# A streaming-encoder step on one core: norms behind a block's second group, w_in scaled on GpSimd from the second group on, latents' transposes in the next block

## The chip, the cores and the metric

The kernel runs on one core of a Trainium2 chip. The metric is the device time of one execution in microseconds, and the time of a kernel is the median of its runs. A core has a matrix engine (TensorE, PE in the profile, with its weight loads as PEld), a vector engine (VectorE, DVE), an activation engine (ScalarE, ACT), a general engine (GpSimd, POOL) and a queue engine that issues DMAs (SyncE, SP). Each engine works through its own instructions in program order and waits on semaphores for the others.

## The reference, cut to what matters

One layer of a hybrid encoder: a norm, one input projection, two token mixers (a gated linear recurrence and latent attention), an output projection, then a feed-forward part. 2048 prompt tokens and 32 tokens of a running stream go through it together. The first half of `trunk_layer` is what the change touches:

```python
xn = rms_norm(x, g_pre_mix)
proj = jnp.einsum('btd,dc->btc', xn, w_in)
x_lru, gate, c_q, c_kv, k_r = jnp.split(
    proj, [LRU_W, 2 * LRU_W, 2 * LRU_W + Q_LORA, 2 * LRU_W + Q_LORA + KV_LORA], axis=-1)

xc, conv_new = causal_conv(x_lru, conv0, conv_w, conv_b)
h, h_last = rglru(xc, h0, w_a, b_a, w_i, b_i, lam)
y_lru = h * jax.nn.gelu(gate)
...
q = jnp.einsum('btr,rhe->bthe', rms_norm(c_q, g_q), w_uq)
ckv_new = rms_norm(c_kv, g_kv)
krope_new = apply_rope(k_r, cos, sin)
```

with

```python
def rms_norm(x, g):
    xf = x.astype(jnp.float32)
    y = xf * lax.rsqrt(jnp.mean(xf * xf, axis=-1, keepdims=True) + EPS)
    return (y * g.astype(jnp.float32)).astype(x.dtype)

# rglru, per channel c and token t:
#   a = exp(-8 * sigmoid(gate r) * softplus(-lam))
#   bx = sqrt(1 - a^2) * sigmoid(gate i) * xc
#   h[t] = a[t] * h[t-1] + bx[t]
```

The model width is 1024 (KD = 8 pieces of 128), the recurrence is 512 wide (G = 4 pieces), c_q is 256, c_kv 128 and k_r 32 wide.

## The kernel before

The program has four stages: `front` (the projection, conv and recurrence, lines 227 to 673), attention, the output projection, and the feed-forward part `mlp`. The last is the longest: the page's lines with `x_hi`, `h_hi` and `w_hl` are its.

**Front** works through 8 blocks of TB = 256 tokens, the last with the 32 stream tokens beside it (288). All products are in float32 in three passes of a rounded high part and a low rest (`mm3`, L159, L160, L161; `split` makes the pair, L147, L149, L152). In a block, PE does in this order: eight groups m=0..7 (each 24 matmuls of 128 x 256, weights `wa_hi`, `wa_lo`, tokens `xt_hi`, `xt_lo`) into a PSUM tile `ps` from a pool `pp` of three buffers; the products of the latents into `psr` (two tiles of the same pool); and the gates, eight sets of three matmuls into `psg`.

The norm isn't applied to the tokens but to the product. Per block two `row` tiles are loaded, squared and summed (ACT L306), turned into `rstd` (POOL L167), spread (`rb`, DVE L309), multiplied with a unit matrix on PE (L320, tile `rps`) and copied by ACT into `r_all` (L324): a row of 256 factors on all partitions. The function `stats` does this. `evac` takes a group's `ps` out and frees its buffer: for m < 4 DVE multiplies with `r_all` into `xl` (L550) and the conv follows (one step on POOL, L556, three on DVE, L561); for m >= 4 DVE multiplies into `gt` (L568), and after m=7 ACT applies the gelu. A group's evacuation can't start before `r_all` is there.

After the groups: `operand` splits the conv's result (`xch`, `xcl`), `latents` takes c_q, c_kv and k_r out of `psr`, with norms (`qn` L389, `kv` L392), and hands back a function `lat_t`, which transposes them on PE (four transposes, L418, into `tps`, a single PSUM buffer), has ACT copy them into `sp_t` (L420) and stores that. `gates` ends in sigmoids on ACT (L456). `recur` runs on ACT (exp L468, tanh L470, Square L471, Sqrt L475, with table loads between), DVE (L472, L483, scans L486) and POOL (L480); `mix` multiplies `gt` with the scan's result (DVE L498) and stores `ylru_d`.

**What sets the order.** PE's order is the order in which the code issues its work; the other engines' orders are made by a scheduler from that program. Before, `gates` of a block issues `stats` of the next block after its third set (j=2) and the first `lat_t` after its fifth (j=4); the second `lat_t` comes after group m=0 of the next block. For block 0 there is no block before: its `rstd` is made while w_in is loaded, and `stats` stands after group m=2; `held` keeps the groups until then.

**Loading w_in** happens during block 0. `load_wa(m)` loads one group's 128 x 1024 weights and has to multiply them by the norm's gain `g_pre`. For m >= 4 GpSimd does that in one instruction (L332), and ACT and DVE split the result in one instruction each (L147, L152). For m < 4 ACT (L341) and DVE (L342) do both at once in eight pieces of 128 x 128 each.

In `mlp`, two PSUM tiles are taken from the pool `pm` and never used ahead of the first products (L1521).

Of the kernel before, what the change touches and what calls it, by code (L numbers as in the profile page):

```python
# [18 lines left out]
KD = 8  # L19
# [15 lines left out]
TB = 256  # L35
# [73 lines left out]
class Step:  # L109
# [117 lines left out]
    def front(self, ca, cb):  # L227
# [3 lines left out]
        with ExitStack() as ctx:  # L231
# [39 lines left out]
            def size(b):  # L271
                return TB + (S if b == self.nb - 1 else 0)
# [24 lines left out]
            def row(i, tag=None):  # L297
                m = 128 if i < self.nt else S
                xr = (tp if tag else rp).tile([128, D], F32, name="xrow_t", tag=tag or "xr")
                nc.sync.dma_start(out=xr[:m], in_=A["x_rows"][i * 128 : i * 128 + m] if m == 128 else A["xs_rows"])  # L300
                return xr
# [10 lines left out]
            def stats(b, rbs=None):  # L312

                n = size(b)
                rps = pr.tile([128, 512], F32, name="rps", tag="rps")
                for t in range((n + 127) // 128):
                    m = min(128, n - t * 128)
                    i = 2 * b + t
                    rb = rbs[t] if rbs else rstd(i, row(i))
                    nc.tensor.matmul(  # L320
                        out=rps[:, t * 128 : t * 128 + m], lhsT=rb[:m], rhs=self.ident[:m, :m], start=True, stop=True
                    )
                r = t2.tile([128, TB + S], F32, name="r_all", tag="r_all")
                nc.scalar.activation(out=r[:, :n], in_=rps[:, :n], func=AF.Copy)  # L324
                return r


            def load_wa(m):
                raw = tp.tile([128, KD, 128], F32, name="wa_raw_t", tag=("ig", "rg", "xcl", "xch")[m % 4])
                nc.sync.dma_start(out=raw, in_=A["w_a"][m])  # L330
                if m >= 4:
                    nc.gpsimd.tensor_tensor(  # L332
                        out=raw, in0=raw, in1=self.g_pre[:, :, None].to_broadcast([128, KD, 128]), op=ALU.mult
                    )
                    self.split(wa_hi[m], wa_lo[m], raw, nc.scalar, nc.vector)
                else:
                    return lambda k: scale_wa(m, k, raw)
# [108 lines left out]
            def gates(w, we, xch, xcl, between={}):  # L446
                rg = tp.tile([128, G, xpad], F32, name="rg", tag="rg")
                ig = tp.tile([128, G, xpad], F32, name="ig", tag="ig")
                for i, (dst, bias) in enumerate(((rg, self.b_a), (ig, self.b_i))):
                    for g in range(G):  # L450
                        ps = pg.tile([128, 512], F32, name="psg", tag="psg")
                        j = i * G + g
                        self.mm3(
                            ps[:, :we], wg_hi[:, j], wg_lo[:, j], xch[:, g, :we], xcl[:, g, :we], True, True
                        )
                        nc.scalar.activation(  # L456
                            out=dst[:, g, :w], in_=ps[:, :w], func=AF.Sigmoid, bias=bias[:, g : g + 1]
                        )
                        if j in between:
                            between[j]()  # L460
                return rg, ig
# [50 lines left out]
            late = []  # L512
            xl_prev = None
            nxt = None
            for b in range(self.nb):
                end = b == self.nb - 1
                n = size(b)
                w = TB + (S + 3 if end else 0)
                we = w + (w % 2)
                if b == 0:  # L520
                    piece = load_wa(0)
                    xh, xlo = load_x(0, 4, piece)
                    piece = load_wa(1)
                    for k in range(KD):
                        piece(k)
                    rows0 = [row(0), row(1, "gt")]
                    rbs = [rstd(i, xr) for i, xr in enumerate(rows0)]
                    for m in (2, 3):
                        piece = load_wa(m)
                        for k in range(KD) if piece else ():  # L530
                            piece(k)
                    r_all = None
                else:
                    xh, xlo = nxt
                    r_all = r_next
                xl = t2.tile([128, G, 3 + xpad], F32, name="xl", tag="xl")
                if b == 0:
                    nc.vector.memset(xl[:, :, 0:3], 0.0)
# [37 lines left out]
                for m in range(8):  # L576
                    if b == 0 and 2 <= m < 6:
                        load_wa(m + 2)
                    if b == 0 and m == 7:
                        load_wb()  # L580
                        wg_raw = t2.tile([128, 2 * G, 128], F32, name="wg_raw", tag="sp_t", bufs=1)
                        nc.sync.dma_start(out=wg_raw, in_=A["w_gate"].rearrange("p a g c -> p (a g) c"))
                        with self.tc.issue_after(self.split(wg_hi, wg_lo, wg_raw, nc.scalar, nc.vector).ins):
                            decay()
                    ps = pp.tile([128, 512], F32, name="ps", tag="ps")
                    for k in range(KD):
                        self.mm3(
                            ps[:, :n], wa_hi[m][:, k], wa_lo[m][:, k], xh[:, k, :n], xlo[:, k, :n],
                            k == 0, k == KD - 1,
                        )  # L590
                    if late and m == 0:
                        late.pop(0)()
                    held.append((m, ps))
                    if r_all is None and m == 2:
                        r_all = stats(0, rbs)
                    if r_all is not None:
                        for x in held:
                            evac(*x)
                        held.clear()
                    if end and m == 6:  # L600

                        hv = recur(end, w, xc, *gates(w, we, *operand(xc, w, we)))
# [23 lines left out]
                if not end:  # L626
                    xch, xcl = operand(xc, w, we)
# [6 lines left out]
                if end:  # L634
                    self.kdone = min(2, (self.n - TB) // 512)
                    t0 = self.nt - TB // 128
                    first = []

                    def early_q(x, ps):

                        self.mul_q(ps, self.uq0, 512 * x)
                        qf = t2.tile([128, 512], F32, name="qf", tag="sp_t", bufs=1)
                        q = [self.k_hi[2][:, 512 * y : 512 * y + 512] for y in (2 * x, 2 * x + 1)]
                        self.first_q[0, x] = self.put_q(ps, 512 * x, qf, *q)

                    def early_k(x, ps):
                        self.mul_k(ps, x, uk)
                        self.put_k(ps, 0, x)

                    self.first_q = {}  # L650
                    t14 = latents(t0, 0, xh, xlo, None)
                    if self.kdone:
                        early_q(0, pr.tile([128, 512], F32, name="psq", tag="rps"))
                        early_k(0, pt.tile([128, 4, 128], F32, name="psk", tag="tps").rearrange("p a b -> p (a b)"))
                    ts = latents(self.nt, TB, xh, xlo, None)
                    t14()
                    t15 = latents(t0 + 1, 128, xh, xlo, None)
                    ts()
                    if self.kdone == 2:
                        early_k(1, pg.tile([128, 512], F32, name="psk", tag="psg"))  # L660
                        early_q(1, pp.tile([128, 512], F32, name="psq", tag="ps"))
                    t15()
                else:
                    sp_t = t2.tile([128, 4, TB], F32, name="sp_t", tag="sp_t", bufs=1)
                    for t in range(n // 128):
                        late.append(latents(2 * b + t, 128 * t, xh, xlo, sp_t))
                    rn = []
                    others = [lambda: rn.append(stats(b + 1)), lambda: late.pop(0)()]
                    rg, ig = gates(w, we, xch, xcl, dict(zip((2, 4), others)))
                    r_next = rn[0]  # L670
                    while len(late) > 1:
                        late.pop(0)()
                    mix(b, end, n, w, xl, gt, recur(end, w, xc, rg, ig))

    def alloc_a(self, ca):
# [829 lines left out]
    def mlp(self):  # L1505
# [11 lines left out]
        g_post = self.cp.tile([128, D], F32, name="g_mlp_post", tag="keep")  # L1517
        nc.sync.dma_start(out=g_post, in_=A["g_rows"][:, D : 2 * D].to_broadcast([128, D]))
        bank = lambda: pm.tile([128, 512], F32, name="ps", tag="ps")

        bank(), bank()  # L1521
        fill, fin = [], []
        turn = [0]
        done = {}
# [385 lines left out]
```

## Time and profile before

| what | us |
|---|---|
| median of 3 runs | 2483.93 |
| the runs | 2483.0 to 2487.58 |
| the profiled execution | 2484.81 |
| its span | 2483.0 |
| end of the front stage in it, about | 352 |

The profile is one execution. A row of the timeline has a start, a duration, an engine, a line, the operation, what it writes and reads, and how often it runs in a row; a bracket tells how long the engine was idle before it and what released it. A row of the waits tells engine, tile and line, what it waited for, and then microseconds in total, times and the longest. A row of the windows has a stretch, its length, and the busy time of PE, PEld, DVE, ACT and POOL with instruction counts, then the clock granted to TensorE (1.00 is full), the DMA engines' share and GB/s.

### The profile page before, as it was taken

The page shows a single profiled execution, that of the slowest core. Times are in us where ns is not written, and L with a number is a line of the kernel's source. Part 1 is how long each engine was busy: PE and PEld are TensorE (multiplying, and loading weights), DVE is VectorE, ACT ScalarE, POOL GpSimd, SP SyncE. Part 2 cuts the span into 40 slices and gives each one's busy share as a digit, 9 for nine tenths or more (in the row PEclk, how much of TensorE's full clock was granted, in tenths as well). Part 3 has the DMA queues.
Part 4 walks back from the last instruction along what each step waited for, and adds up shares of the span by engine and source line. Part 5 has one row for each costly group of instructions (what it writes and reads, how often), then busy time and mean ns, then how long its engine had stood idle before and what let it go on. Part 6 is the DMA issues. An engine that isn't in the chain of part 4 may idle for free.

```text
span 2483.0 us, 44188 instructions
## 1 busy us (share of the span) xinstructions
PE 2391.4 (96%) x15287; PEld 2274.4 (92%) x15287; DVE 1788.7 (72%) x3573; ACT 1549.9 (62%) x3473; POOL 624.2 (25%) x1040
## 2 busy tenths in 40 slices
PE   7999989999999999999999999999999999999998
PEld 7889978888888787777999999999999999999997
DVE  7646589898888884465877777676677777667676
ACT  6554558788788783343666766466676656666564
POOL 4443366777577682111000000000000000000000
PEclk9999999999999999999999999999999999999999
DMA  6522211333334325495666887676678767667773
GB/s 211 146 73 75 79 49 50 84 84 87 86 86 123 99 59 164 121 288 171 210 221 227 282 261 242 210 239 232 215 268 261 241 218 236 226 230 267 236 240 131
DMA packets 325489, 436.45 MB, mean 176 GB/s; under 512 B 32336, under 2 KB 242544, under 8 KB 325264
## 3 DMA queue, kind: packets, MB, share of 16 engines
q1 hardware_dynamic: 324624, 433.10, 54.8%
q8 instruction: 120, 1.97, 0.3%
q14 instruction: 105, 0.86, 0.1%
q10 hardware_dynamic: 640, 0.52, 0.1%
HBM read 309.63 MB, written 123.90 MB: 175 GB/s over the span
## 4 chain that ended last, share of the span: by engine, by line
PE 71%; DVE 10%; ACT 6%; issue 5%; POOL 4%; DMA 2%; SPq 0%; ACTq 0%; DVEq 0%; POOLq 0%
PE ps L159 17%; PE ps L160 17%; PE ps L161 17%; PE po L995 4%; PE ptp L979 4%; PE pss L159 2%; PE pss L160 2%; PE pss L161 2%; DVE xc L561 1%; ACT w_hl L147 1%; ACT p L913 1%; DVE w_hl L152 1%; DVE hv L486 1%; DVE c L1619 1%; POOL xc L556 1%
## 5 line engine op out<-in xcount | busy, mean ns | idle before, releaser
L159 PE MATMUL ps<-x_hi,w_hl 128*128 128x352 f32 (+1 forms) x1344 | 432.4, 322 | 5.0 <-DVE x L1387 3.3
L160 PE MATMUL ps<-x_lo,w_hl 128*128 128x352 f32 (+1 forms) x1344 | 432.4, 322 | 0.0
L159 PE MATMUL ps<-h_hi,w_hl 128*128 128x352 f32 (+1 forms) x1344 | 432.3, 322 | 0.0
L161 PE MATMUL ps<-x_hi,w_hl 128*128 128x352 f32 (+1 forms) x1344 | 431.5, 321 | 0.0
L160 PE MATMUL ps<-h_lo,w_hl 128*128 128x352 f32 (+1 forms) x1344 | 430.4, 320 | 0.1
L161 PE MATMUL ps<-h_hi,w_hl 128*128 128x352 f32 (+1 forms) x1344 | 430.4, 320 | 0.0
L1717 POOL TENSOR_TENSOR rs<-rs,neg_half 128x1 f32<-128x1 f32 (+2 forms) x18 | 14.3, 796 | 1283.6 <-DVE rs L1711 1228.3
L147 ACT ACTIVATE h_hi<-h_raw 128x352 fp32r<-128x352 f32 (+1 forms) x336 | 165.1, 492 | 212.1 <-PE ps L160 205.3
L152 DVE TENSOR_TENSOR h_lo<-h_raw,h_hi 128x352 fp32r<-128x352 f32 (+1 forms) x336 | 173.5, 517 | 144.0 <-ACT h_hi L147 140.6
L159 PEld LDWEIGHTS ps<-x_hi,w_hl 128*128 128x128 f32 x1344 | 253.1, 188 | 6.1 <-issue 3.5
L160 PEld LDWEIGHTS ps<-x_lo,w_hl 128*128 128x128 f32 x1344 | 253.3, 188 | 0.0
L161 PEld LDWEIGHTS ps<-x_hi,w_hl 128*128 128x128 f32 x1344 | 253.3, 188 | 0.0
L160 PEld LDWEIGHTS ps<-h_lo,w_hl 128*128 128x128 f32 x1344 | 252.4, 188 | 0.4 <-DVE h_lo L152 0.4
L159 PEld LDWEIGHTS ps<-h_hi,w_hl 128*128 128x128 f32 x1344 | 252.4, 188 | 0.1
L161 PEld LDWEIGHTS ps<-h_hi,w_hl 128*128 128x128 f32 x1344 | 252.4, 188 | 0.0
L940 POOL TENSOR_SCALAR p<-p,r,e 128x512 f32<-128x512 f32 (+2 forms) x288 | 203.1, 718 | 111.8 <-DVE r L938 68.3
L913 ACT ACTIVATE p<-pss,nm 128x512 f32<-128x512 f32 (+2 forms) x320 | 198.8, 623 | 36.7 <-DVE nm L909 30.2
L983 DVE TENSOR_TENSOR pt_lo<-ptp,pt_hi 128x512 fp32r<-128x512 f32 (+1 forms) x288 | 187.7, 655 | 28.3 <-ACT pt_hi L982 24.1
L152 DVE TENSOR_TENSOR w_hl<-wd_raw,w_hl 128x512 fp32r<-128x512 f32 x288 | 197.8, 689 | 4.4 <-ACT w_hl L147 3.1
L982 ACT ACTIVATE pt_hi<-ptp 128x512 fp32r<-128x512 f32 (+1 forms) x288 | 163.8, 573 | 55.2 <-PE ptp L979 51.2
L909 DVE TENSOR_REDUCE nm<-pss 128x1 f32<-128x512 f32 (+2 forms) x320 | 188.8, 600 | 9.4 <-PE pss L161 6.9
L1600 ACT ACTIVATE c<-c 128x352 f32<-128x352 f32 (+1 forms) x144 | 71.0, 493 | 198.1 <-DVE c L1599 198.1
(493 smaller groups left out, 6006.2 us busy)
## 6 DMA issues: line engine op xcount, KB each, us to landing
wu_raw<-w_up SPq DMA_DIRECT2D x96, 512.0 KB, 4.2
wd_raw<-ws_d SPq DMA_DIRECT2D x96, 512.0 KB, 4.3
h_d<-c SPq DMA_DIRECT2D x224, 176.0 KB, 3.3
h_raw<-h_d SPq DMA_DIRECT2D x112, 352.0 KB, 4.1
wd_raw<-w_down SPq DMA_DIRECT2D x72, 512.0 KB, 4.4
h_d<-c SPq DMA_DIRECT2D x112, 168.0 KB, 3.4
h_raw<-h_d SPq DMA_DIRECT2D x56, 336.0 KB, 4.1
wsum<-w_down SPq DMA_DIRECT2D x128, 128.0 KB, 2.6
```

The lines of the kernel that those rows point to most:

```text
L147: r = nc.scalar.activation(out=hi, in_=src, func=AF.Copy)
L152: self.low = le.tensor_sub(lo, src, hi.bitcast(F32))
L159: mm(out=out, lhsT=ah, rhs=bh, start=first, stop=False, skip_group_check=more)
L160: mm(out=out, lhsT=ah, rhs=bl, start=False, stop=False, skip_group_check=more)
L161: mm(out=out, lhsT=al, rhs=bh, start=False, stop=last, skip_group_check=more)
L909: nc.vector.tensor_reduce(out=nm[:, c1], in_=ps[:, :ln], axis=AX.X, op=ALU.max, negate=True)
L913: nc.scalar.activation(out=p[:, :ln], in_=ps[:, :ln], func=AF.Exp, bias=nm[:, c1], scale=1.0, accum_out=ls[:, c1],)
L940: self.seen = nc.gpsimd.tensor_scalar(out=p[:, : k1 - k0], in0=p[:, : k1 - k0], scalar1=r, scalar2=0.0 if e is None else e[:, x : x + 1], ...
L979: nc.tensor.transpose(out=pt[:, 128 * x : 128 * x + 128], in_=blk(o[1], o[0]), identity=self.ident)
L982: nc.scalar.activation(out=hi[:, c0:], in_=pt[:, c0:], func=AF.Copy)
L983: nc.vector.tensor_sub(lo[:, c0:], pt[:, c0:], hi[:, c0:].bitcast(F32))
L995: nc.tensor.matmul(out=po, lhsT=vv, rhs=part[:, 256 * x : 256 * x + 256], start=(u == 0 and x + y == 0), stop=(u == j and x + y == 2),)
```

## The change

Four edits:

1. A function `ahead(b)` is called where `stats(b)` was, in the gates after j=2. For a block of plain size it makes only the `rstd` part; the norm's matmuls and `r_all` are made by `stats` after group m=1 of the block itself, in block 0 as well (there it stood after m=2). The last, wider block keeps all of `stats` in the gates.
2. No latents' transposes stand in the gates any more: one is done after group m=0 of the next block and one after m=1, ahead of the norm's matmuls.
3. GpSimd scales w_in for m >= 1 (before: m >= 4).
4. The two unused tiles in `mlp` are no longer taken. The banks that its tiles get, and the order of its instructions, are the same as before.

```diff
+            def ahead(b):
+
+                if size(b) > TB:
+                    return stats(b), None
+                return None, [rstd(i, row(i)) for i in (2 * b, 2 * b + 1)]
 
             def load_wa(m):
...
-                if m >= 4:
+                if m >= 1:
                     nc.gpsimd.tensor_tensor(
...
-                    piece = load_wa(1)
-                    for k in range(KD):
-                        piece(k)
+                    load_wa(1)
                     rows0 = [row(0), row(1, "gt")]
                     rbs = [rstd(i, xr) for i, xr in enumerate(rows0)]
                     for m in (2, 3):
-                        piece = load_wa(m)
-                        for k in range(KD) if piece else ():
-                            piece(k)
+                        load_wa(m)
                     r_all = None
                 else:
                     xh, xlo = nxt
-                    r_all = r_next
+                    r_all, rbs = r_next
...
-                    if late and m == 0:
+                    if late:
                         late.pop(0)()
                     held.append((m, ps))
-                    if r_all is None and m == 2:
-                        r_all = stats(0, rbs)
+                    if r_all is None and m == 1:
+                        r_all = stats(b, rbs)
...
                     rn = []
-                    others = [lambda: rn.append(stats(b + 1)), lambda: late.pop(0)()]
-                    rg, ig = gates(w, we, xch, xcl, dict(zip((2, 4), others)))
+                    rg, ig = gates(w, we, xch, xcl, {2: lambda: rn.append(ahead(b + 1))})
                     r_next = rn[0]
-                    while len(late) > 1:
-                        late.pop(0)()
                     mix(b, end, n, w, xl, gt, recur(end, w, xc, rg, ig))
...
         bank = lambda: pm.tile([128, 512], F32, name="ps", tag="ps")
-
-        bank(), bank()
```

ACT's instructions from the gates of block 3 to the gelu of block 4, before (`rg` and `ig` are the gates' sigmoids, `a_...` the recurrence's factor, `sp_t` the transposed latents):

```order
L456 ACTIVATE rg<-psg,cols 128x256 x2
L324 ACTIVATE r_all<-rps 128x256
L456 ACTIVATE rg<-psg,cols 128x256
L456 ACTIVATE ig<-psg,cols 128x256
L420 ACTIVATE sp_t<-tps 128x4x128
L456 ACTIVATE ig<-psg,cols 128x256 x3
L468 ACT_TABLE_LOAD
L468 ACTIVATE av<-rg,cneg 128x256 x4
L470 ACTIVATE rg<-rg,cpos 128x256 x4
L471 ACTIVATE a_2238<-av 128x4x256
L420 ACTIVATE sp_t<-tps 128x4x128
L475 ACT_TABLE_LOAD
```

and the same stretch in the changed kernel:

```order
L462 ACTIVATE rg<-psg,cols 128x256 x3
L462 ACTIVATE ig<-psg,cols 128x256 x4
L474 ACT_TABLE_LOAD
L474 ACTIVATE av<-rg,cneg 128x256 x4
L476 ACTIVATE rg<-rg,cpos 128x256 x4
L477 ACTIVATE a_2188<-av 128x4x256
L426 ACTIVATE sp_t<-tps 128x4x128 x2
L481 ACT_TABLE_LOAD
L481 ACTIVATE a_2188<-a_2188 128x4x256
L324 ACTIVATE r_all<-rps 128x256
L572 ACT_TABLE_LOAD
```

The copy of `r_all` and the first `sp_t` copy have left the sigmoids; both copies now stand between the recurrence's Square (now L477) and the table load ahead of its Sqrt (now L481), and `r_all` behind the Sqrt.

DVE's instructions at the start of block 4, before, from the spreading of the norm's factors to the evacuation of group m=3:

```order
L309 COPY rb<-rstd 128x128 x2
L550 TENSOR_TENSOR xl<-ps,r_all 128x256
L561 SCALAR_TENSOR_TENSOR xc<-xl,cols,xc 128x256 x3
L550 TENSOR_TENSOR xl<-ps,r_all 128x256
L472 SCALAR_TENSOR_TENSOR a_2238<-a_2238,rg 128x4x256
L561 SCALAR_TENSOR_TENSOR xc<-xl,cols,xc 128x256 x3
L550 TENSOR_TENSOR xl<-ps,r_all 128x256
L561 SCALAR_TENSOR_TENSOR xc<-xl,cols,xc 128x256
L483 TENSOR_TENSOR ig<-ig,a_2238 128x4x256
L561 SCALAR_TENSOR_TENSOR xc<-xl,cols,xc 128x256
L486 SCALAR_TENSOR_TENSOR hv<-av,hlast,ig 128x256 x4
```

and in the changed kernel, up to the evacuation of group m=2:

```order
L478 SCALAR_TENSOR_TENSOR a_2188<-a_2188,rg 128x4x256
L309 COPY rb<-rstd 128x128 x2
L489 TENSOR_TENSOR ig<-ig,a_2188 128x4x256
L552 TENSOR_TENSOR xl<-ps,r_all 128x256
L492 SCALAR_TENSOR_TENSOR hv<-av,hlast,ig 128x256 x4
L563 SCALAR_TENSOR_TENSOR xc<-xl,cols,xc 128x256
L500 COPY hlast<-hv 128x4
L504 TENSOR_TENSOR gt<-gt,hv 128x4x256
L563 SCALAR_TENSOR_TENSOR xc<-xl,cols,xc 128x256
L552 TENSOR_TENSOR xl<-ps,r_all 128x256
L563 SCALAR_TENSOR_TENSOR xc<-xl,cols,xc 128x256
L552 TENSOR_TENSOR xl<-ps,r_all 128x256
```

Before, three evacuations (`xl`) stood ahead of the multiplication of `ig`, which reads the Sqrt's result, and of the scans; now the first evacuation stands behind that multiplication and the second behind the scans and the multiplication of `gt`.

GpSimd's instructions in block 0, from the tokens' split on, before:

```order
L149 TENSOR_SCALAR xt_hi<-xt_raw_t 128x512 x4
L167 TENSOR_TENSOR rstd<-rstd,neg_half 128x1 x2
L332 TENSOR_TENSOR wa_raw_t<-wa_raw_t,cols 128x1024 x3
L556 TENSOR_SCALAR xc<-xl,cols 128x256 x3
L332 TENSOR_TENSOR wa_raw_t<-wa_raw_t,cols 128x1024
L556 TENSOR_SCALAR xc<-xl,cols 128x256
```

and in the changed kernel:

```order
L149 TENSOR_SCALAR xt_hi<-xt_raw_t 128x512 x4
L338 TENSOR_TENSOR wa_raw_t<-wa_raw_t,cols 128x1024
L167 TENSOR_TENSOR rstd<-rstd,neg_half 128x1 x2
L338 TENSOR_TENSOR wa_raw_t<-wa_raw_t,cols 128x1024 x4
L558 TENSOR_SCALAR xc<-xl,cols 128x256 x2
L338 TENSOR_TENSOR wa_raw_t<-wa_raw_t,cols 128x1024 x2
L558 TENSOR_SCALAR xc<-xl,cols 128x256 x2
```

Seven scalings stand where four stood: one ahead of the powers that make `rstd`, four ahead of the first two conv steps.

## The prediction

> **What bounds the kernel now.** I read the page first: busy shares, slices, the chain that ended last.
>
> ```profile
> span 2483.0 us, 44188 instructions
> PE 2391.4 (96%) x15287; PEld 2274.4 (92%) x15287; DVE 1788.7 (72%) x3573; ACT 1549.9 (62%) x3473; POOL 624.2 (25%) x1040
> PE   7999989999999999999999999999999999999998
> PE 71%; DVE 10%; ACT 6%; issue 5%; POOL 4%; DMA 2%; SPq 0%; ACTq 0%; DVEq 0%; POOLq 0%
> ```
>
> TensorE is the bound: busy in 96% of the span, thinnest in the first slice. The changed front stage is the first 352 us, and everything behind it waits for TensorE's order, so an idle microsecond taken from PE there, or added, moves the end by as much. Next I asked for what PE waits on up to 352 us (in total, times, longest), and then for PE's busy time by stretches that hold one block boundary each (into blocks 2, 3, 4, 5 and 6).
>
> ```profile
> PE tps L418 <- DVE qn L389: 7.4, 4, 3.2
> PE psg L159 <- ACT rg L456: 3.6, 7, 1.1
> PE ps L159 <- DVE xl L550: 2.7, 1, 2.7
> PE ps L159 <- DVE gt L568: 2.5, 3, 2.0
> PE ps L161 <- DVE wa_lo L342: 1.7, 2, 1.1
> ...
> 84.00:124.00 40.00, 37.76 (x284) 36.95 (x282) 22.39 (x52) 25.14 (x49) 19.73 (x26) 1.00 0.50 145
> 124.00:164.00 40.00, 37.02 (x277) 36.20 (x276) 21.63 (x47) 22.84 (x45) 18.32 (x25) 1.00 0.36 109
> 164.00:202.50 38.50, 35.76 (x255) 35.09 (x255) 20.00 (x40) 18.58 (x37) 14.20 (x19) 0.96 0.15 48
> 202.50:240.00 37.50, 36.68 (x277) 36.00 (x277) 21.44 (x43) 18.57 (x37) 14.92 (x20) 1.00 0.23 67
> 240.00:280.00 40.00, 38.65 (x293) 37.99 (x293) 23.20 (x48) 18.57 (x37) 16.16 (x20) 1.00 0.18 59
> ```
>
> The first two columns give PE's idle time: 2.24, 2.98, 2.74, 0.82 and 1.35 us, 10.13 in five boundaries. A boundary costs little already; the most that the change can take there is about 10 us. The windows also show the granted clock (the column behind POOL):
>
> ```profile
> 24.00:27.40 3.40, 1.69 (x8) 1.69 (x9) 2.32 (x5) 0.33 (x1) 1.53 (x1) 0.50 0.70 186
> ...
> 164.00:166.00 2.00, 0.11 (x1) 0.00 (x0) 0.39 (x2) 0.42 (x1) 1.92 (x2) 1.00 0.01 2
> ...
> 168.00:170.00 2.00, 2.00 (x12) 2.00 (x11) 0.00 (x0) 0.00 (x0) 0.00 (x0) 0.50 0.00 0
> ```
>
> After the 2.7 us wait for xl, and after the 2.0 us wait for gt just ahead of 166, PE runs at 0.50: twelve matmuls in 2.00 us, where the stretch from 202.5 on has 277 in 37.5. From 84 to 164 the clock stays 1.00 although the three other waits for qn average (7.4 - 3.2) / 3 = 1.4 us. So between 1.4 and 2.0 us of idle the clock halves; a halved stretch of 3.4 us (the first row's 24.0 to 27.4) does half its work, which loses 1.7 us. With the one such loss the five boundaries cost 10.13 + 1.7 = 11.8 us.
>
> The Trainium skill ("TensorE: Matmul & The Clock Gate", Part 1: The HAM clock gate) lets the clock fall after an idle window of about 3.4 us and calls the window free-running, 3413 ns long. The row of 2.0 us of idle followed by 0.50 contradicts the first; by the page's rule none of the waits below would cost clock, and the forecast would be 3.4 us lower.
>
> **Norms and transposes, the steady boundary.** Before, the norm matmul L320 and the copy r_all L324 ran among the gates, so the next block's evacuations had r_all early. Now they stand behind the second group, and both latents' transposes too. The rows of the boundary into block 4, PE, ACT, DVE:
>
> ```profile
> 180.69 0.61 PE L320 MATMUL rps<-ident,rb 128*128 128x128 f32 x4
> 181.05 0.36 PE L159 MATMUL psg<-xch,wg_hi 128*128 128x256 f32 x1
> ...
> 185.72 0.28 PE L159 MATMUL ps<-xt_hi,wa_hi 128*128 128x256 f32 x1
> 185.84 0.28 PE L160 MATMUL ps<-xt_lo,wa_hi 128*128 128x256 f32 x1
> ...
> 182.15 0.40 ACT L324 ACTIVATE r_all<-rps 128x256 f32<-128x256 f32 x1
> 182.41 0.50 ACT L456 ACTIVATE rg<-psg,cols 128x256 f32<-128x256 f32 x1
> ...
> 183.12 0.64 ACT L420 ACTIVATE sp_t<-tps 128x512 f32<-128x512 f32 x1
> 183.60 1.25 ACT L456 ACTIVATE ig<-psg,cols 128x256 f32<-128x256 f32 x3
> ...
> 189.38 1.05 ACT L471 ACTIVATE a<-av 128x1024 f32<-128x1024 f32 x1
> 190.33 0.57 ACT L420 ACTIVATE sp_t<-tps 128x512 f32<-128x512 f32 x1
> 190.92 1.28 ACT L475 ACT_TABLE_LOAD   x1
> 192.59 1.06 ACT L475 ACTIVATE a<-a 128x1024 f32<-128x1024 f32 x1 [0.39 <-DVE a L472]
> ...
> 187.79 0.41 DVE L550 TENSOR_TENSOR xl<-ps,r_all 128x256 f32<-128x256 f32 x1
> ...
> 195.98 1.22 DVE L483 TENSOR_TENSOR ig<-ig,a 128x1024 f32<-128x1024 f32 x1
> ...
> 197.51 2.67 DVE L486 TENSOR_TENSOR_SCAN hv<-av,hlast,ig 128x256 f32<-128x256 f32 x4
> 200.10 0.46 DVE L561 SCALAR_TENSOR_TENSOR xc<-xl,cols,xc 128x256 f32<-128x256 f32 x1
> ...
> 200.55 1.22 DVE L498 TENSOR_TENSOR gt<-gt,hv 128x1024 f32<-128x1024 f32 x1
> 201.68 0.42 DVE L550 TENSOR_TENSOR xl<-ps,r_all 128x256 f32<-128x256 f32 x1
> ```
>
> A matmul follows the last by 0.12 us (185.72 to 185.84), so a group of 24 takes 2.88; the norm's matmuls take 0.36 (180.69 to 181.05); a set of four transposes I set at 0.45. On DVE xl of m=0 was done by 188.2, long before the fourth group needs one of the three PSUM buffers.
>
> Now, with the same durations. ACT is rid of r_all (182.15 to 182.41, 0.26) and one sp_t copy (183.12 to 183.60, 0.48) among the sigmoids, so its Square ends 0.74 earlier, at 189.7. The first sp_t copy waits behind that Square, ends at 190.2, and only then may PE write the second transposes into the single tps buffer: PE, done with m=1 at about 190.1, hardly waits. From there ACT's row is: second copy 0.57, table load 1.28, Sqrt 1.06, r_all; DVE's is ig (L483, which waits for Sqrt), then xl of m=0. From the second transposes: 0.45 + 0.57 + 1.28 + 1.06 + 1.22 + 0.41 = 5.0 us until xl of m=0 has freed a buffer, 5.1 with the hand-overs. PE has behind that point 0.45 + 0.36 + 2.88 = 3.7. **The fourth group waits 1.4 to 1.5 us.**
>
> Then DVE's scans stand ahead of xl of m=1: scans 2.59 (197.51 to 200.10), two conv steps at 0.4, the hlast copy and gt multiplication 1.2, xl 0.42, about 5.0 us. PE has one group, 2.88. **The fifth group waits 2.1 us**; from then on DVE has nothing long ahead of an evacuation. With about 0.5 us of gate and transpose waits (one gate wait a block stays: 3.6 / 7) a boundary costs 1.5 + 2.1 + 0.5 = 4.1 us, five cost 20.5 against 11.8: **+8.7**.
>
> What goes: the waits of transposes for qn (they now stand a whole group later) and the gt wait, whose store starts earlier relative to the groups. Both are in the 11.8. What is late next is r_all itself and the scans.
>
> The last boundary keeps its norm among the gates (the block is wider); its transposes move: +0.1, from 0 to 0.5.
>
> **Clock.** A 2.1 us wait lies just above the 2.0 that halved the clock, but only if it falls in one stretch of 3.4 us: (3.4 - 2.1) / 3.4 = 0.38, two of the six boundaries into blocks 1 to 6, 2 x 1.7 = **+3.4**. From below this is 0, from above six, 10.2.
>
> **Block 0 and the boundary into block 1.** GpSimd takes the scaling of three more groups; 24 DVE and 24 ACT pieces become three wide ones each.
>
> ```profile
> 13.30 2.18 DVE L342 SCALAR_TENSOR_TENSOR wa_lo<-wa_raw_t,cols,wa_hi 128x128 fp32r<-128x128 f32 x8
> 16.88 7.31 DVE L342 SCALAR_TENSOR_TENSOR wa_lo<-wa_raw_t,cols,wa_hi 128x128 fp32r<-128x128 f32 x15
> ...
> 33.30 1.21 DVE L152 TENSOR_TENSOR wa_lo<-wa_raw_t,wa_hi 128x1024 fp32r<-128x1024 f32 x1
> ...
> 20.04 1.90 POOL L332 TENSOR_TENSOR wa_raw_t<-wa_raw_t,cols 128x1024 f32<-128x1024 f32 x1 [0.53 <-ACT wa_hi L341]
> ```
>
> Eight pieces take 2.18, 0.27 each; fifteen beside two GpSimd scalings took 7.31 instead of 4.1, so each scaling holds DVE up by 1.6 us. DVE saves 24 x 0.27 - 3 x 1.21 = 2.9 and loses 3 x 1.6 = 4.8: 1.9 more by m=5 to m=7, whose lo parts come from these scalings. Against it stand the wa_lo waits (1.7) and the xl wait (2.7, with 1.7 of clock): r_all is asked for one group earlier, so buffers come free sooner. If nothing held DVE up the stage would save about 6 (all three); if all of its scalings met DVE it loses 4. I take +1.3, nearest to the rows of shared time: block 0 ends about 2.9 later, and the boundary into block 1, where today's 3.2 us wait for qn goes and the two steady waits come, gives 1.6 back.
>
> The Trainium skill ("SBUF — State Buffer", SBUF: two separate sides) says that GpSimd and a DVE operation with two SBUF inputs lock each other out for a whole instruction. By that each scaling would cost up to its 1.9 us, 0.9 more in all than by the rows' 1.6.
>
> **The dropped banks in the last stage** shift no bank that is used and no order; the first product's wait there stays. Nothing.
>
> **Sum.** 8.7 + 0.1 + 3.4 + 1.3 = 13.5 us. The profiled execution took 2484.81 us (1.8 of it outside the span), 0.9 above the median 2483.93: 2498.3 against the profile, 2497.4 against the median; I say 2498.
>
> **Rivals.**
> - *Waits come, the clock holds, and block 0 gains its 6.* For it: 1.4 us of idle left the clock at 1.00, and 2.1 is barely over the 2.0 seen once. Against it: the 7.31 row. 8.7 + 0.1 - 6 = +2.8, 2487.
> - *The clock falls at all six boundaries.* For it: GpSimd's conv beside DVE's conv steps can stretch the 2.1 to 2.6. 13.5 + 6.8 + 6 x 0.5 = +23, 2507.
> - *Faster: r_all late but hidden.* Its point of decision: the 5.0 us from the second transposes to xl of m=0 must fit into PE's 3.7, and the 5.0 to xl of m=1 into 2.9. If the engines' queues let xl of m=0 past L483 and the scans (or the store and Sqrt come 1.5 to 2 us earlier than the rows say), the fourth and fifth groups start at once; then the boundaries keep 0.5 each, 2.5 - 11.8 = -9.3, with block 0's -6 it is -15, 2469. Against it: DVE's order is fixed, L483 and the scans are ahead of the two xl.
> - *The change doesn't do what it says*, the transposes only wait elsewhere: that is in the forecast, as the waits for tps move to xl.
>
> **How the numbers follow.** Forecast 0.62 (2490 to 2506), the second rival 0.12, the first 0.16, the faster one 0.10. The range takes in the first two rivals: 2486 to 2510, leaving out most of the faster case and a tail. Under 0.2% (5 us) can't be told from no change: faster 0.09, same 0.16, slower 0.75.
>
> **What would show it.** Right: waits of PE's ps L159 for DVE xl, two in each of blocks 1 to 6, about 1.5 and 2.1 us; no wait of tps for qn; two or more new stretches at clock 0.50; some 3 to 4 us more idle in each stretch of one boundary; in block 0 DVE rows drawn out beside GpSimd's scalings. Wrong: fourth and fifth groups that start at once; a Sqrt that ends before PE's second transposes; a block 0 in which m=5 to m=7 wait for nothing; a first product of the last stage that waits differently.

## The result, and the profile after

The changed kernel takes **2512.48 us** (3 runs, 2511.93 to 2514.79) against 2483.93 before (2483.0 to 2487.58): ratio 1.0107, 95% interval 1.0093 to 1.0121. It is slower, as forecast, but by 28.5 us where 14 were said, and outside the range, which ended at 2510. The profiled execution took 2511.93 us, 27.1 more than the one before.

The page of the changed kernel, its span, busy times and the chain that ended last:

```profile
span 2510.1 us, 44151 instructions
PE 2401.0 (96%) x15287; PEld 2281.3 (91%) x15287; DVE 1793.0 (71%) x3552; ACT 1548.7 (62%) x3452; POOL 638.9 (25%) x1043
PE 74%; ACT 8%; DVE 8%; issue 4%; DMA 3%; POOL 2%; SPq 0%; ACTq 0%; DVEq 0%; POOLq 0%
```

Averages hardly tell the two kernels apart. One share does: DMA is now 3% of the chain, 2% before. What PE waits on up to 380 us tells more (in total, times, longest):

```profile
PE ps L159 <- DVE xl L552: 22.9, 14, 3.5
PE psg L159 <- ACT rg L462: 10.7, 8, 6.3
...
PE tps L424 <- ACT sp_t L426: 1.9, 4, 0.5
```

Fourteen waits for xl where there was one; one wait of 6.3 us at the gates, which the prediction doesn't have; and the waits of transposes for DVE's qn, 7.4 us in four before, are down to one of 0.8.

Where the time came in is seen from the start of each block (the first matmul of m=0 behind the gates). Lengths from one start to the next, block 0 from the span's start, for the two kernels and, for later use, the experiments:

| block | before | after | E1 | E2 | E3 | E4 | E5 | E6 | E7 | E8 |
|---|---|---|---|---|---|---|---|---|---|---|
| 0 | 58.9 | 60.7 | 58.7 | 62.2 | 58.3 | 59.9 | 60.9 | 60.8 | 59.7 | 58.3 |
| 1 | 42.6 | **49.1** | 42.8 | 42.7 | 41.3 | 42.8 | 43.1 | 48.7 | 42.2 | 41.3 |
| 2 | 40.2 | 41.6 | 41.5 | 39.8 | 38.6 | 42.0 | 41.9 | 41.6 | 39.6 | 37.8 |
| 3 | 42.2 | 43.2 | 43.2 | 40.7 | 37.6 | 38.1 | 43.2 | 39.4 | 39.4 | 37.6 |
| 4 | 37.8 | **41.8** | 41.9 | 37.7 | 37.8 | 38.3 | 41.8 | 39.6 | 39.5 | 37.8 |
| 5 | 37.6 | **41.7** | 41.9 | 37.6 | 37.6 | 38.5 | 43.2 | 39.4 | 39.4 | 37.6 |
| 6 | 39.0 | **44.1** | 44.1 | 39.0 | 38.4 | 39.3 | 42.6 | 40.3 | 40.3 | 38.4 |

Of the 27.1 us, block 0 has 1.8, block 1 6.5, blocks 2 to 6 together 15.6, block 7 0.4, and 2.9 lie behind the front stage.

**A steady boundary**, into block 4. First the timeline of PE around the fourth and fifth groups, then ACT's and DVE's:

```profile
205.03 0.28 PE L161 MATMUL ps<-xt_hi,wa_lo 128*128 128x256 f32 x1
206.71 0.38 PE L159 MATMUL ps<-xt_hi,wa_hi 128*128 128x256 f32 x1 [1.41 <-DVE xl L552]
206.93 0.28 PE L160 MATMUL ps<-xt_lo,wa_hi 128*128 128x256 f32 x1
...
211.71 0.39 PE L159 MATMUL ps<-xt_hi,wa_hi 128*128 128x256 f32 x1 [1.85 <-DVE xl L552]
```

```profile
200.71 0.57 ACT L426 ACTIVATE sp_t<-tps 128x512 f32<-128x512 f32 x1
202.03 0.60 ACT L426 ACTIVATE sp_t<-tps 128x512 f32<-128x512 f32 x1 [0.75 <-PE tps L424]
202.64 1.28 ACT L481 ACT_TABLE_LOAD   x1
203.94 1.06 ACT L481 ACTIVATE a<-a 128x1024 f32<-128x1024 f32 x1
204.90 0.37 ACT L324 ACTIVATE r_all<-rps 128x256 f32<-128x256 f32 x1
```

```profile
205.10 1.22 DVE L489 TENSOR_TENSOR ig<-ig,a 128x1024 f32<-128x1024 f32 x1 [2.40 <-ACT a L481]
206.24 0.42 DVE L552 TENSOR_TENSOR xl<-ps,r_all 128x256 f32<-128x256 f32 x1
206.58 2.77 DVE L492 TENSOR_TENSOR_SCAN hv<-av,hlast,ig 128x256 f32<-128x256 f32 x4
...
209.72 1.21 DVE L504 TENSOR_TENSOR gt<-gt,hv 128x1024 f32<-128x1024 f32 x1
...
211.25 0.41 DVE L552 TENSOR_TENSOR xl<-ps,r_all 128x256 f32<-128x256 f32 x1
```

This is the chain of the prediction, link for link: both copies, table, Sqrt, r_all; then ig, one xl, the scans, gt, the next xl. The fourth group waits 1.41 (said: 1.4 to 1.5), the fifth 1.85 (2.1). It repeats in every block from 3 to 6.

**Block 1's gates.** What stands in ACT's queue from the row loads of block 1 to the gates of its end, and when the first of those loads was issued on SP:

```profile
69.06 1.98 SPq L284 DMA_DIRECT2D xt_raw_t<-x_t  x2
71.13 0.45 SPq L300 DMA_DIRECT2D xrow_t<-x_rows  x1
...
79.18 1.06 ACT L306 ACTIVATE xrow_t<-xrow_t 128x1024 f32<-128x1024 f32 x1 [7.21 <-DMA xrow_t<-x_rows]
...
84.64 1.06 ACT L306 ACTIVATE xrow_t<-xrow_t 128x1024 f32<-128x1024 f32 x1 [4.32 <-DMA xrow_t<-x_rows]
...
89.58 1.06 ACT L306 ACTIVATE xrow_t<-xrow_t 128x1024 f32<-128x1024 f32 x1 [3.79 <-DMA xrow_t<-x_rows]
...
99.23 1.06 ACT L306 ACTIVATE xrow_t<-xrow_t 128x1024 f32<-128x1024 f32 x1 [1.30 <-DMA xrow_t<-x_rows]
...
103.99 1.06 ACT L306 ACTIVATE xrow_t<-xrow_t 128x1024 f32<-128x1024 f32 x1 [0.77 <-DMA xrow_t<-x_rows]
...
105.04 0.59 ACT L379 ACTIVATE pr__1218<-psr,rstd 128x416 f32<-128x416 f32 x1
...
106.05 0.58 PE L159 MATMUL psg<-xch,wg_hi 128*128 128x256 f32 x1 [6.28 <-ACT rg L462]
```

Each row Square (six; the one at 94.41 isn't shown) waits for its own load into the one row buffer, and the next load can't start before that Square is done: about 4.9 us a piece. The second copy of the latents, L379, and the gates' sigmoids stand behind the sixth. PE had run out of psg buffers at 99.8 and waits until 106.05.

Before, there are five such Squares. The first starts 6.2 us earlier, and the same matmul of the gates hardly waits; the first and the last Square, the copy behind it and that matmul:

```profile
72.96 1.07 ACT L306 ACTIVATE xrow_t<-xrow_t 128x1024 f32<-128x1024 f32 x1 [0.21 <-DMA xrow_t<-x_rows]
...
96.45 1.06 ACT L306 ACTIVATE xrow_t<-xrow_t 128x1024 f32<-128x1024 f32 x1 [0.89 <-DMA xrow_t<-x_rows]
97.51 0.59 ACT L373 ACTIVATE pr__1257<-psr,rstd 128x416 f32<-128x416 f32 x1
...
99.56 0.39 PE L159 MATMUL psg<-xch,wg_hi 128*128 128x256 f32 x1 [0.39 <-ACT rg L456]
```

### The profile page after: what moved, and what is told of

Same layout as the page of the kernel before. It is cut to its first block, busy times and chain, and to the rows that moved or that the text cites. A ratio compares the mean times of both kernels' runs of the same rounds, so it can differ in the third digit from the quotient of the medians.

```text
span 2510.1 us, 44151 instructions
## 1 busy us (share of the span) xinstructions
PE 2401.0 (96%) x15287; PEld 2281.3 (91%) x15287; DVE 1793.0 (71%) x3552; ACT 1548.7 (62%) x3452; POOL 638.9 (25%) x1043
## 4 chain that ended last, share of the span: by engine, by line
PE 74%; ACT 8%; DVE 8%; issue 4%; DMA 3%; POOL 2%; SPq 0%; ACTq 0%; DVEq 0%; POOLq 0%
PE ps L159 18%; PE ps L160 18%; PE ps L161 18%; PE po L994 4%; PE ptp L978 4%; PE pss L159 2%; PE pss L160 2%; PE pss L161 2%; DMA xrow_t<-x_rows 1%; ACT w_hl L147 1%; ACT p L912 1%; DVE w_hl L152 1%; DVE c L1616 1%; ACT c L1597 1%; ACT pt_hi L981 1%
## 5 line engine op out<-in xcount | busy, mean ns | idle before, releaser
L152 DVE TENSOR_TENSOR h_lo<-h_raw,h_hi 128x352 fp32r<-128x352 f32 (+1 forms) x336 | 173.4, 517 | 146.9 <-ACT h_hi L147 141.6
L152 DVE TENSOR_TENSOR w_hl<-wd_raw,w_hl 128x512 fp32r<-128x512 f32 x288 | 197.9, 689 | 4.3 <-ACT w_hl L147 3.1
```

The lines of the kernel that those rows point to most:

```text
L152: self.low = le.tensor_sub(lo, src, hi.bitcast(F32))
```

## The experiments

The changed kernel differs from before by three edits that move something: norms (edit 1), transposes (edit 2) and the scaling (edit 3). The first four kernels take them apart. All ratios are to the kernel before.

**E1, without the scaling.**

```diff
-                if m >= 1:
+                if m >= 4:
                     nc.gpsimd.tensor_tensor(
...
-                    load_wa(1)
+                    piece = load_wa(1)
+                    for k in range(KD):
+                        piece(k)
```

> The changed kernel with w_in scaled as before (GpSimd from the fifth group on). Theory: the two waits for xl (about 1.4 and 1.9 us a boundary) and the long wait of block 1's gates (6.3 us) come from the other two edits and stay; 2505 to 2511 us. Rival: GpSimd's scalings make block 0 late, the row loads behind it too, and so the gates' wait of block 1; then the wait is under 1 us here, block 0 and block 1 give back 8 us, and the time is 2504 or less.

Measured: 2504.36 us, ratio 1.0083 (1.0068 to 1.0098), 8.1 less than the changed kernel. The waits for xl stay (1.4 and 1.9 in blocks 3 to 6), but the gates of block 1 wait 0.43. So on that wait the rival was right and the theory, in this form, wrong: the six Squares are there in E1 too. ACT's timeline of E1 shows the difference, the first of the six and the copy behind the last:

```profile
72.10 1.06 ACT L306 ACTIVATE xrow_t<-xrow_t 128x1024 f32<-128x1024 f32 x1 [2.56 <-DMA xrow_t<-x_rows]
...
96.27 1.06 ACT L306 ACTIVATE xrow_t<-xrow_t 128x1024 f32<-128x1024 f32 x1 [0.69 <-DMA xrow_t<-x_rows]
...
97.75 0.61 ACT L379 ACTIVATE pr__1257<-psr,rstd 128x416 f32<-128x416 f32 x1 [0.32 <-PE psr L161]
```

The chain is as long, but starts 7.1 us earlier (72.10 against 79.18) and ends just before it is needed. Of the 7.1, 4.7 are a later issue on SP (71.13 in the changed kernel, 66.44 in E1); the rest is that first load itself, 8.0 us from issue to landing against 5.6. On SP it stands behind two token loads, which go out when DVE's split (L152) has read their buffer out. In the changed kernel that split stands behind the latents' norm, in E1, as before, ahead of it; why the scheduler turned the two around wasn't traced. DVE in the changed kernel, and in E1:

```profile
65.10 2.48 DVE L395 TENSOR_SCALAR qn<-pr__774,rs 128x256 f32<-128x256 f32 x1 [0.48 <-POOL rs L392]
...
67.77 1.21 DVE L152 TENSOR_TENSOR xt_lo<-xt_raw_t,xt_hi 128x1024 fp32r<-128x1024 f32 x1
```

```profile
61.46 1.22 DVE L152 TENSOR_TENSOR xt_lo<-xt_raw_t,xt_hi 128x1024 fp32r<-128x1024 f32 x1
62.60 2.50 DVE L395 TENSOR_SCALAR qn<-pr__813,rs 128x256 f32<-128x256 f32 x1
```

**E2, the scaling alone** (the same edit made to the kernel before).

> The kernel before with GpSimd's scaling from the second group on, and nothing else. Theory: block 0 ends about 2 us later, block 1's gates wait for nothing new: 2484 to 2487 us. Rival (scaling at the root of block 1's loss): plus 8, 2492.

Measured: 2489.20 us, ratio 1.0017 (1.0008 to 1.0027), so 3.7 us, between the two expectations. Block 0 is 3.3 longer, with one wait for xl of 5.5 us; block 1's gates wait 0.32. Alone, the scaling has no part in block 1.

**E3, the transposes alone.**

```diff
-                    if late and m == 0:
+                    if late:
                         late.pop(0)()
...
-                    others = [lambda: rn.append(stats(b + 1)), lambda: late.pop(0)()]
-                    rg, ig = gates(w, we, xch, xcl, dict(zip((2, 4), others)))
+                    rg, ig = gates(w, we, xch, xcl, {2: lambda: rn.append(stats(b + 1))})
                     r_next = rn[0]
-                    while len(late) > 1:
-                        late.pop(0)()
```

> The kernel before with both latents' transposes in the next block, the norm's matmuls still in the gates. Theory: r_all is there early, so no waits for xl; the waits of transposes for qn (3.2, 1.6, 1.6 us) go: 2477 to 2482 us. Rival: the transposes' copies alone delay ACT's Sqrt and with it the evacuations; waits of 1 us and more for xl, 2490 or more.

Measured: **2478.79 us**, ratio 0.9975 (0.9966 to 0.9985). In all blocks behind block 0 there is one wait for xl, 1.1 us in block 1, and none for DVE's qn; blocks 2 and 3 get 1.6 and 4.6 us shorter. This is faster than both kernels.

**E4, the norms alone** (edit 1, with the first transposes behind the fifth set of gates as before; the unused banks of edit 4 are dropped too).

> The kernel before with the norm's matmuls behind group m=1, transposes as before. Theory: r_all's copy stands ahead of the Sqrt, so groups four and five wait under 0.5 us each, but ACT has the sixth row Square ahead of block 1's latents as in the changed kernel, so block 1's gates wait 4 to 6 us: 2489 to 2495 us. Rival: the late norm alone makes the waits for xl: 2498 or more.

Measured: 2488.51 us, ratio 1.0014 (1.0004 to 1.0023). Blocks 3 to 6 have no wait for xl at all, 38.1 to 39.3 us long; in blocks 1 and 2 three such waits stay (1.7, 0.6, 1.9). The gates of block 1 wait 0.9, not 4 to 6: there the theory missed again, for the same reason as in E1 (six Squares, the first at 73.54). Against the kernel before in the same comparison (2485.49) the three edits alone give +3.7, -6.7 and +3.0 us, which adds to nothing; together they cost 27 (2512.48 against 2485.49). The loss is in how they meet.

**E5, the rows held back.** Only the order in which the scheduler places the row loads and Squares is changed; it puts three Squares ahead of block 1's latents where six stood, and two a block later on.

```diff
+                        if m == 3:
+                            mark.append(e.ins)
...
-                return None, [rstd(i, row(i)) for i in (2 * b, 2 * b + 1)]
+                with self.tc.issue_after(mark[-1]):
+                    return None, [rstd(i, row(i)) for i in (2 * b, 2 * b + 1)]
```

(`e` is the evacuation of a group; the last block's `stats` is held in the same way.)

> The changed kernel, but the row loads and Squares of the next block's norm may start only after this block's fourth evacuation. Theory: block 1's gates wait 6.3 us because ACT works off six row Squares, each behind a load into the one row buffer, ahead of the latents' copies; held back there are three, the wait falls under 1 us, and the kernel gains 7 to 9 us: 2503 to 2506 us. The waits for xl (1.4 and 1.9) stay. Rival (GpSimd's scaling makes DVE and block 1 late by itself): the wait stays at 4 us or more, 2510 or more.

Measured: 2505.93 us, ratio 1.0086 (1.0072 to 1.0099), 6.6 us less than the changed kernel. In the timeline of its PE the wait of 6.28 is this:

```profile
102.37 0.39 PE L159 MATMUL psg<-xch,wg_hi 128*128 128x256 f32 x1 [0.43 <-ACT rg L464]
```

The scaling is all there, block 0 as long as in the changed kernel, and the wait is gone. With E1 this makes it two conditions: a chain of six loads, and a late start. The late start needs the scaling (without it, in E1 and E4, the first Square starts at 72.10 and 73.54); either condition alone, in E1 or in E5, leaves a wait of 0.43 at these gates.

**E6, the norm first.** The norm gets priority in the scheduler.

```diff
-                        r_all = stats(b, rbs)
+                        with self.tc.high_priority(2000):
+                            r_all = stats(b, rbs)
```

ACT's order at the boundary into block 4 becomes

```
L426 ACTIVATE sp_t<-tps 128x4x128 x2
L324 ACTIVATE r_all<-rps 128x256
L481 ACT_TABLE_LOAD
L481 ACTIVATE a_2188<-a_2188 128x4x256
```

and DVE has two evacuations ahead of ig, two behind the scans. Into blocks 1 and 2 the order stays.

> The changed kernel with the norm given priority in the scheduler, which puts r_all's copy ahead of the recurrence's table load and Sqrt, and two evacuations ahead of the multiplication of ig, in blocks 3 to 6; blocks 1 and 2 keep the order of the changed kernel. Theory: in blocks 3 to 6 the waits of 1.4 and 1.9 us go (third evacuation behind the scans: a wait of 0.3 at most), in blocks 1 and 2 they stay; 14 us less, and up to 3 for the clock: 2495 to 2500 us. Rival (the transposes' place or r_all's lateness as such makes the waits): half of them or more stay, 2505 or more.

Measured: 2499.23 us, ratio 1.0056 (1.0041 to 1.0071), 13.3 us less. In blocks 3 to 6 both waits are gone, in blocks 1 and 2 they stay. A new one came, larger than the 0.3 allowed, at the sixth group:

```profile
208.23 0.39 PE L159 MATMUL ps<-xt_hi,wa_hi 128*128 128x256 f32 x1 [1.22 <-DVE xl L552]
```

The third evacuation still stands behind the scans and gt. So it was the place of r_all behind the Sqrt, and with it two evacuations, that made the two waits; one wait of 1.2 to 1.3 is left of 3.3.

**E7, rows held back and the norm first.**

> The changed kernel with both repairs: rows held back and the norm first (from block 2 on). Theory: the gains add, 7 to 9 and 15 to 20 us; 2484 to 2490 us, within 0.3 percent of before. Rival (something else in the change costs time): 2493 or more.

Measured: 2490.97 us, ratio 1.0023 (1.0014 to 1.0032), 21.5 less than the changed kernel and one microsecond above the expected end. With these orders alone, all three edits in place, three quarters of the loss are gone. What is left against before is block 0 (0.8) and blocks 4 to 6 (4.9, of which the sixth groups' waits are 3.7), less a gain of 3.9 in blocks 1 to 3, and the clock behind the front stage.

**E8, E3 with the rows held back.**

> The kernel before with both transposes in the next block, norm's matmuls in the gates, and the rows held back as above. Theory: against the same kernel without the holding back (2478.8) block 1's waits for the row's Square (1.6 us, transposes) and for the gates (1.2 us) go: 2474 to 2478 us. Rival: the rows come too late for the norm in the gates, waits of rps for rb, 2480 or more.

Measured: 2479.52 us, ratio 0.9974 (0.9964 to 0.9984): the same as E3, and the gain didn't come. Of the two waits that it aimed at, the gates' is down (1.2 to 0.3), but a new one of 1.26 for DVE's gt came in block 1. The other, for the Square, is still there, since the scheduler left that one Square where it was:

```profile
66.08 0.41 PE L422 MATMUL tps<-ident,qn 128*128 128x128 f32 x2 [1.54 <-ACT xrow_t L306]
```

**E9 and E10, both kernels profiled once more.**

> The kernel before, unchanged, profiled once more. Theory: where the stretches of halved clock lie is a matter of each execution, since the 3.41 us grid doesn't start with the kernel; between 400 and 1175 us this profile shows 2 to 4 halved stretches where the first showed none, and takes 3 to 7 us longer there. Rival: the halved stretches belong to the program; again none there.

> The changed kernel, unchanged, profiled once more. Theory: the waits of PE in the front stage repeat within 0.3 us each (6.3 at block 1's gates, 1.4 and 1.9 a boundary), while the stretches of halved clock fall at other boundaries than into blocks 3 and 6, one to four of them. Rival: the same boundaries again.

E9 took 2489.39 us, 4.6 more than the first profile of the same kernel. The same stretches in both, windows of the first profile and of E9 (the clock is the third number from the end):

```profile
863.68:867.10 3.42, 3.19 (x22) 2.77 (x22) 3.31 (x11) 3.10 (x10) 0.00 (x0) 1.00 0.38 143
897.82:901.23 3.41, 3.41 (x26) 3.19 (x25) 2.87 (x8) 3.00 (x10) 3.41 (x4) 1.00 0.32 86
1007.04:1010.46 3.42, 3.42 (x22) 2.97 (x21) 0.69 (x1) 1.75 (x2) 0.20 (x1) 1.00 0.02 7
```

```profile
863.68:867.10 3.42, 3.42 (x11) 2.34 (x12) 3.31 (x8) 2.01 (x6) 0.00 (x0) 0.55 0.65 209
897.82:901.23 3.41, 3.35 (x16) 3.29 (x16) 0.97 (x2) 1.52 (x4) 3.33 (x5) 0.55 0.27 77
1007.04:1010.46 3.42, 2.63 (x8) 2.25 (x9) 0.85 (x2) 1.59 (x3) 3.30 (x6) 0.55 0.91 306
```

Between 400 and 1175 us these are three halved stretches where the first profile had none; the changed kernel has three there in both its profiles, and those of E1 to E8 have two to four up to 1150 us. So the 2.9 us that it lost behind the front stage are of the kind that the kernel before loses too in some executions, and most likely not the change's work: only that first profile lacks them. In the front stage the second half of E10's expectation failed: E10 (2509.90 us) has its halved stretches at the same boundaries as the first profile, behind the gates' wait into block 2 and in blocks 3 and 6. Its waits for xl repeat within 0.1 us from block 3 on; the gates of block 1 wait 4.8 instead of 6.3.

## Why the prediction was right on the two waits and wrong on the sum

**The two waits for xl: right in mechanism, place and size.** 1.41 and 1.85 to 1.89 us in blocks 3 to 6, against 1.4 to 1.5 and 2.1. E4 and E3 show that neither edit makes them alone, E6 that they hang on r_all behind the Sqrt, as the prediction had it.

**Their cost: about 0.7 us a boundary too small.** The prediction said 4.1 us a boundary against the idle time of before. Idle time after is 4.12 in block 4 (two xl waits, 0.43 each at transposes and gates), yet the block is 4.08 longer than before's with its 0.78 idle, not 3.34. The PE rows above show a part of it: from 205.03 to 206.71 are 1.68 us, where a matmul otherwise follows after 0.12, and the next one comes 0.22 behind; 1.66 lost where the row says 1.41. A wait costs a quarter of a microsecond more than its idle time, and a boundary has two more of them than before. The remaining quarter was not traced. Over blocks 2 to 6 the term of 8.7 and 3.4, 12.1 together, measured 15.6. The idle time itself came out as said: waits of PE over 0.25 us in these blocks are 9.9 us before and 20.3 after, where the prediction had 10.1 and 20.5. What it put at nothing is the rest: seven more waits at a quarter each make 1.8, and at the start of block 2 the clock is still at 0.50 for 2.0 us behind the gates' wait, which is 1.0; 0.7 stays open.

**Clock: right in number, with luck.** Two of the six boundaries lost clock behind their xl waits, as said: one behind the wait at 168.54, one behind 295.21. A third, into block 2, lost it behind the gates' wait, which the prediction doesn't have. Its reason for two, a chance of 0.38 at each boundary, isn't shown: E10 has the same two again. And its threshold doesn't hold. It put the waits for qn that left the clock at 1.00 at 1.4 us, but the smallest of the three averaged, 0.96, lies ahead of 84 us, and the two in its stretch are 1.58 and 1.62. In E3 waits of 0.32 and 1.23 within 3.4 us were enough, and in block 1 of the changed kernel one of 1.91 wasn't. E5 gives a price: its block 6 has the same waits without a halved stretch and is 1.5 us shorter, near the 1.7 that was used.

**Block 0 and the boundary into block 1: right in size up to block 1's latents.** Block 0's latents start 2.95 us later (46.55 against 43.60; said: 2.9), block 1's 1.40 later (89.53 against 88.13; said: 1.3 in all). That the scaling does it is shown by E1, where block 0's latents start at 43.65. DVE is held up beside GpSimd, as the prediction said: two splits of 1.21 take 4.65 in all while GpSimd scales.

```profile
17.88 9.44 POOL L338 TENSOR_TENSOR wa_raw_t<-wa_raw_t,cols 128x1024 f32<-128x1024 f32 x4
...
20.91 4.65 DVE L152 TENSOR_TENSOR wa_lo<-wa_raw_t,wa_hi 128x1024 fp32r<-128x1024 f32 x2 [1.05 <-ACT wa_hi L147]
```

But the term was a choice between 6 saved and 4 lost, and the wait for xl that it set against the loss didn't shrink (2.74 before, 3.50 after), so its closeness is in part luck.

**What failed: the gate wait behind block 1.** The sum has "about 0.5 us of gate and transpose waits" at every boundary, from 3.6 / 7 before, as if nothing ahead of the gates' sigmoids on ACT changed but r_all and one sp_t copy, which leave. At the boundary into block 2 the gates wait 6.28 us. The prediction never follows the other instructions of the moved step, the row loads and the Squares on ACT, which no longer stand under `stats` but are issued by `ahead`. The scheduler put one more of them into block 1 (six for five), and the first load of that chain went out on SP behind token loads that block 0's delay and DVE's new order had made late. E1 and E5 each take one of the two conditions away, and the wait with it. Where block 1's latents begin the kernel had lost 1.4 us; at the start of block 2, with the halved clock behind the wait, it had lost 8.3. This term is half of the miss (about 7 of 13.6); the waits' cost beyond their idle time and the clock at the start of block 2 (3.5) and the halved stretches behind the front stage (2.9) are nearly all of the rest. Its size is that of one execution: E10 has 4.79 at the same place, E6 5.05.

**What goes: right.** The waits for DVE's qn and for gt behind its store are gone from the list, but for one of 0.8. The unused banks: the first product of the last stage waits 3.3 us for x in both profiles. **The faster rival** was refuted for this order; E3 shows where the gain was: with the transposes moved and r_all left among the gates, the old waits go and no new ones come. E4 shows the same from the other side, with no wait for xl in blocks 3 to 6.

## What to carry to other kernels

When a step is moved, list everything it issues, the loads that feed it too, and look at what stands behind each in its engine's queue: when an engine works off loads through one buffer in order, whatever stands behind them waits too (here 6.28 us). Two moves that are harmless alone can meet in one queue; try each alone before they are put together, and keep the one that pays (here the transposes, 0.9975). When a long function like the recurrence stands ahead of a result that several evacuations wait for, look where the scheduler puts that result: here priority for r_all was worth 13.3 us.

## What the runs showed of the hardware that was not expected

- A wait of PE that the profile gives as 1.41 us of idle moved the next matmuls by 1.66.
- A wait of 1.86 us was enough to halve the clock for one stretch (behind 295.21, where the clock is 0.54 from 296.5 to 299.8), and waits of 1.85 to 1.91 at four other boundaries weren't. In the front stage the waits in blocks 3 and 6 were hit in both profiles of the changed kernel; behind it the number of halved stretches between 400 and 1175 us differed between two profiles of the kernel before, none and three.

This is the window behind that wait:

```profile
296.50:299.80 3.30, 3.30 (x19) 3.30 (x18) 3.27 (x9) 1.28 (x1) 1.25 (x2) 0.54 0.12 41
```

In block 0 of E3 less was enough. In the first of these two windows PE waits 0.32 and 1.23 us and is busy for 1.85 of 3.40, and in the second the clock is halved:

```profile
19.10:22.50 3.40, 1.85 (x14) 1.48 (x13) 3.40 (x8) 1.96 (x5) 2.00 (x2) 1.00 0.01 2
22.50:25.90 3.40, 2.62 (x14) 2.33 (x12) 3.40 (x11) 0.74 (x2) 0.00 (x0) 0.52 0.56 149
```

The Trainium skill ("TensorE: Matmul & The Clock Gate", Part 1: The HAM clock gate) has the clock fall after an idle window of about 3.4 us. These runs don't agree: 1.86 us were enough, if not each time, and in E3 0.32 and 1.23 together, so the measurement is what to plan by.
